# A hybrid attention, DeltaNet and gated-MLP layer on one core: modulation products, load queues and the second norm rearranged

## The chip, the cores and the metric

The kernel runs on one core of one Trainium2 chip. Its time is the device time of one execution in microseconds (us), and the time given for a kernel is the median over several runs. Engines are named as in the profile: PE is TensorE (matmuls, with weight loads as PEld), DVE is VectorE, ACT is ScalarE, POOL is GpSimd, SP is SyncE, which only issues transfers here. SPq and ACTq are the issuing queues of SP and ACT.

## The reference

One layer of a diffusion backbone, on 256 latent tokens x and 256 context tokens ctx of width 2048. A conditioning vector (c for the latents, c_ctx for the context) gives six modulation vectors through one matrix, w_ada (2048 x 12288). What bears on this case:

```python
sh1, sc1, g1, sh2, sc2, g2 = split(silu(c) @ w_ada + b_ada, 6)
csh1, csc1, ...            = split(silu(c_ctx) @ w_ada + b_ada, 6)
lat = modulate(rmsnorm(x, norm_mix), sh1, sc1) @ w_in       # modulate: h * (1 + scale) + shift
con = modulate(rmsnorm(ctx, norm_mix), csh1, csc1) @ w_in
# columns of lat, con feed latent attention (8 heads) and a bidirectional gated DeltaNet (8 heads)
y = (sigmoid(gate_a) * (y_mla @ w_o_mla) + sigmoid(gate_b) * (y_dn @ w_o_dn)) @ w_out
x = x + g1 * y
h = modulate(rmsnorm(x, norm_ffn), sh2, sc2)
gate, val = split(h @ w_ffn_up, 2)                          # hidden width 5504
x = x + g2 * ((silu(conv3(gate)) * val) @ w_ffn_down)
```

Of the modulation, only the first two vectors (shift sh1, scale sc1) are needed for both streams; g1, sh2, sc2 and g2 are needed for the latents alone.

## The kernel before

Activations lie transposed: features on the 128 partitions, tokens along the free axis, so a width of 2048 is 16 tiles (k = 0 to 15) of 128 x 256 per stream. Every large product is done with operands split in two parts of less precision (hi and lo: ACT rounds, DVE subtracts, lines 119 and 120) and three partial products. Weights come from HBM into tiles of tag raw, 128 x 1024 words, of which there are five (NR = 5) for the whole kernel.

**The opening** (lines 313 to 490) computes the first modulated norm H and at the same time the first projection `fp`, seven column groups of w_in (864 columns, `wfirst`), accumulated over k in seven PSUM tiles. It is written out by hand: PE, ACT (`oact`) and DVE (`odve`) keep the order of the program there. SP's loads are issued in the order written, each when its buffer is free.

- `spread` copies silu(c) and silu(c_ctx) to all partitions (`scb`), by 16 matmuls for each stream and copies by DVE (latents) and ACT (context).
- The squares of x and ctx are summed over features on PE (`pss`), gathered (`part`, `msp`), raised to -1/2 on POOL (`rsq`, L171) and spread over partitions by four matmuls (`bc_ps`, then `bc`). Tiles of squares, the output that the DVE reductions throw away (`junk`) and `part` share tag sq, two buffers.
- Shift columns: the 16 feature tiles make 8 pairs. For pair p four raw tiles are loaded (`load_shift`, L333), multiplied on PE with silu(c), silu(c_ctx) as 32 columns (`mod_mm`: 32 matmul instructions, tile `amp`, and an ACT copy `row`), summed into columns by PE and finished with the bias by ACT (`mod_cols`, tile `shs`).
- Scale columns (`aas`): for the pairs in SCP the same way from the `wt` tiles; for the other feature tiles two DVE reductions each (`scale_dot`, one per stream, 128 x 2048) and one ACT instruction (`scale_fin`). `dots` names the tile of the loop behind which each reduction stands. There are three `wt` buffers of 1 MB.
- Tile k of the loop at L461: the product of a pair of columns for two tiles ahead, the rounding of the next weights (`first_hi`), the matmuls of the seven groups (`first_mm`, 42 for each k) with the column sums between them, the reductions, the next tile of H (`h_prep`), then the loads for k + 4. In tile 1 ACT issues a store of the latents' spread vector to HBM (`Sc`, 1 MB).

**The other modulation vectors** (g1, sh2, sc2, g2; `ada_rest`, L258 to 283) are made beside everything that follows: 128 rows of 512 KB (`rawa`, in the five raw tiles), each loaded by SP and reduced by one DVE instruction (L277) against half of the spread vector (`sch`, loaded from `Sc`). The generator is driven by a rate: each step of another stage calls `ada(ns)`, which adds to what is owed, and as long as something is owed the generator goes on by one yield of 1300. At a change of half it yields without work, two times before the load of `sch` and four after it. The rates are ADB (DeltaNet preparation), AD (attention), ADS (scan), WO (per tile of the output projection) and 1000 per tile of the MLP. 32 rows must be done before the output projection's residual (`ada.done` = 1), 96 before the second norm (`while ada.done < 3`, a loop that makes up for what is missing).

**The second norm** (L1360 to 1400): the output projection (`ops`, 16 tiles of 32 matmul pairs) adds up the squares of x1 on DVE (`ssq`, L1373); the sum over partitions, the power and the spread follow as in the opening, all through class `Rms`. `h2_tile` then makes H2 for each k: DVE multiplies by the norm, ACT scales and shifts, ACT rounds, DVE subtracts. The first four tiles of the MLP (`fps`) go through k in quarters, beside h2_tile. From L506 on the order within an engine is set by a planner, apart from a few stretches.

## Time and profile before

| | us |
|---|---|
| median of 3 runs (1857.85 to 1868.06) | 1860.94 |
| the profiled execution, its own time | 1860.39 |
| its span, first to last instruction | 1858.6 |
| PE busy | 1788.5 (96%) |
| DVE busy | 1376.6 (74%) |
| ACT busy | 928.4 (50%) |
| moved by DMA | 419.71 MB, 226 GB/s |

Mean granted clock of PE over the span: 0.990 of full speed. A row of instructions names line, engine, operation, output <- input, count, busy time and mean duration; in a row ordered by time the first number is the start and the second the duration (or the stretch, where instructions are merged), and square brackets give the idle time of the engine before it and what ended it. Lines are those of the kernel; operations that the ordered wrapper issues all carry line 68, so tile names tell them apart. Matmuls are pipelined, so the durations of neighbours overlap.

### The profile page before, as it was taken

The numbers are of one execution on the slowest core, as the hardware profiler recorded it, in microseconds if no ns is written. First come the engines' busy times: TensorE is split into PE (matmuls) and PEld (weight loads), VectorE is DVE, ScalarE is ACT, GpSimd is POOL, SyncE is SP. The second block draws the span as 40 slices with busy tenths as digits, with TensorE's granted clock in tenths as the row PEclk, the third lists the DMA queues.
The fourth block names the chain that finished last, engine by engine and source line by source line (L and its number), as shares of the span: only waits on it lengthen the run. The fifth ranks groups of instructions, "written<-read, shape, count | busy, mean of one in ns | idle before, by whom it ended". The sixth has DMA issues, their size and how long they took to land.

```text
span 1858.6 us, 32954 instructions
## 1 busy us (share of the span) xinstructions
PE 1788.5 (96%) x12386; PEld 1527.4 (82%) x12386; DVE 1376.6 (74%) x2766; ACT 928.4 (50%) x1899; POOL 44.3 (2%) x45
## 2 busy tenths in 40 slices
PE   7899999999999999999999988999999999999999
PEld 4788887888888887778788876888888888888888
DVE  5677889779777876575679888888877788855554
ACT  3335544444666666233346536555555555544443
POOL 0000001000000000000000000000000000000000
PEclk9999999999999999999999998999999999999999
DMA  9992688774677767777757885767766667766663
GB/s 346 342 373 75 178 230 248 202 246 125 207 237 237 224 208 217 260 253 235 244 188 252 293 282 187 251 222 225 224 215 186 211 217 223 263 200 192 196 200 120
DMA packets 195008, 419.71 MB, mean 226 GB/s; under 512 B 61280, under 2 KB 101344, under 8 KB 192416
## 3 DMA queue, kind: packets, MB, share of 16 engines
q1 hardware_dynamic: 167952, 402.39, 67.1%
q10 hardware_dynamic: 26896, 15.21, 2.7%
q8 instruction: 97, 1.59, 0.3%
q14 instruction: 63, 0.52, 0.1%
HBM read 388.57 MB, written 28.84 MB: 225 GB/s over the span
## 4 chain that ended last, share of the span: by engine, by line
PE 54%; DMA 3%; DVE 2%; ACT 1%; issue 1%; POOL 0%; SPq 0%; ACTq 0%; DVEq 0%
PE fps L68 26%; PE dps L68 13%; PE brp L68 5%; PE gtp L68 4%; PE ops L68 3%; DMA rawa<-in_wada 2%; PE op L68 1%; PE kp L68 1%; PE yp L68 1%; DVE wlo L120 1%; DMA raw<-in_wgate 0%; DMA jit<-Vs 0%; DVE rawa L277 0%; DMA yraw<-Ys 0%; DVE S L1284 0%
## 5 line engine op out<-in xcount | busy, mean ns | idle before, releaser
L120 DVE TENSOR_TENSOR wlo<-raw,whi 128x512 fp32r<-128x512 f32 (+1 forms) x940 | 634.0, 686 | 194.5 <-ACT whi L119 185.4
L119 ACT CAST whi<-raw 128x512 fp32r<-128x512 f32 (+1 forms) x940 | 573.9, 619 | 398.4 <-PE dps L68 113.2
L68 PE MATMUL fps<-H,whi 128*128 128x512 f32 x1376 | 481.8, 398 | 5.7 <-DVE H L120 5.7
L68 PE MATMUL fps<-H,wlo 128*128 128x256 f32 x1376 | 374.6, 282 | 0.8 <-DVE wlo L120 0.7
L68 PEld LDWEIGHTS fps<-H,whi 128*128 128x128 f32 x1376 | 253.7, 189 | 62.6 <-issue 5.7
L68 PEld LDWEIGHTS fps<-H,wlo 128*128 128x128 f32 x1376 | 259.2, 188 | 9.4 <-DVE wlo L120 1.9
L68 PE MATMUL gtp<-h,whi 128*128 128x512 f32 x640 | 235.1, 402 | 0.0
L68 PE MATMUL mmp<-h,whi 128*128 128x512 f32 x640 | 228.9, 400 | 0.0
L68 PE MATMUL dps<-GB,whi 128*128 128x512 f32 x560 | 195.9, 391 | 0.0
L277 DVE CUSTOM_DVE_ANT_0 rawa<-rawa,sch 128x1024 f32<-128x1024 f32 x128 | 156.3, 1222 | 49.6 <-DMA rawa<-in_wada 48.6
L68 PE MATMUL gtp<-h,wlo 128*128 128x256 f32 x640 | 175.9, 285 | 1.4 <-DVE wlo L120 1.4
L68 PE MATMUL mmp<-h,wlo 128*128 128x256 f32 x640 | 176.5, 282 | 0.0
L68 PE MATMUL dps<-GB,wlo 128*128 128x256 f32 x560 | 155.3, 282 | 0.0
L68 PEld LDWEIGHTS gtp<-h,whi 128*128 128x128 f32 x640 | 120.7, 189 | 25.5 <-issue 1.2
L68 PEld LDWEIGHTS mmp<-h,whi 128*128 128x128 f32 x640 | 119.1, 188 | 26.2 <-issue 0.4
L68 PEld LDWEIGHTS gtp<-h,wlo 128*128 128x128 f32 x640 | 121.2, 190 | 7.4 <-DVE wlo L120 1.8
L68 PEld LDWEIGHTS dps<-GB,whi 128*128 128x128 f32 x560 | 105.1, 188 | 21.7
L68 PEld LDWEIGHTS mmp<-h,wlo 128*128 128x128 f32 x640 | 120.4, 188 | 2.8 <-issue 0.6
L68 PEld LDWEIGHTS dps<-GB,wlo 128*128 128x128 f32 x560 | 105.9, 189 | 0.6
L68 PE MATMUL fp<-h,gh 128*128 128x256 f32 (+1 forms) x448 | 86.5, 293 | 6.2 <-ACT h L68 5.2
L68 PEld LDWEIGHTS fp<-h,gh 128*128 128x128 f32 (+1 forms) x448 | 70.3, 191 | 12.1 <-ACT h L68 6.4
L496 ACT COPY fx<-fps 128x256 f32<-128x256 f32 x86 | 31.9, 374 | 68.6 <-PE fps L68 68.6
(557 smaller groups left out, 2602.1 us busy)
## 6 DMA issues: line engine op xcount, KB each, us to landing
rawa<-in_wada SPq DMA_DIRECT2D x128, 512.0 KB, 4.6
raw<-in_wgate SPq DMA_DIRECT2D x82, 512.0 KB, 4.3
raw<-in_wval SPq DMA_DIRECT2D x82, 512.0 KB, 4.7
raw<-in_wdown SPq DMA_DIRECT2D x80, 512.0 KB, 4.3
wt<-in_wadas SPq DMA_DIRECT2D x16, 1024.0 KB, 8.0
raw<-in_wadab SPq DMA_DIRECT2D x32, 512.0 KB, 8.1
raw<-in_wgm SPq DMA_DIRECT2D x32, 512.0 KB, 4.8
raw<-in_wgd SPq DMA_DIRECT2D x32, 512.0 KB, 5.2
```

Source lines behind the costliest of these rows:

```text
L68: i = f(*a, **k)
L119: act.copy(hi, raw)
L120: dve.tensor_tensor(out=lo, in0=raw, in1=hi, op=ALU.subtract)
L277: dve.tensor_tensor_reduce(out=w, in0=w, in1=sch, scale=1.0, scalar=0.0, op0=ALU.mult, op1=ALU.add, accum_out=parts[:, h, j : j + 1])
L496: act.copy(out, ps[:M, T:])
```

## The change

In the opening, the order of squares, spreads and reductions is rewritten; a reduction for the second stream writes over its weights instead of a junk tile of tag sq. The product of pair 0 moves ahead of the norm's broadcast. All further products move into the odd tiles of the loop, the scale product at its start and the shift product after the fourth group; four pairs (1, 3, 5, 7) instead of three take the product on PE for the scales, and the host lays out the weights of these pairs accordingly. The shift loads of pairs 1 to 7 are issued by ACT. The store of Sc moves from tile 1 to tile 12, and wt is loaded ahead of the weights of fp in each tile. The second norm sums the last tile's squares on PE instead of on DVE, keeps the scale and the norm in one DVE instruction, and lets ACT write the rounded part at once. The rates ADB, AD and ADS rise, and a change of half takes one and three yields instead of two and four.

```diff
--- before.py
+++ after.py
@@ -29,7 +29,7 @@
 GH = 512
 NR = 5
 NH = 6
-AD = 0.55
+AD = 0.6
 GD0 = 2
 SC = 7500
 ON = 3000
@@ -37,16 +37,16 @@
 CB = 2000
 CC = 7000
 RE = 1.0
-ADS = 0.3
+ADS = 0.4
 OD = 8000
 OC = 4000
 WO = 1500
 IK = 7000
 NW = 3
-SCP = (2, 5, 7)
+SCP = (1, 3, 5, 7)
 R0 = 1.3
 R1 = 1.0
-ADB = 4000
+ADB = 4500
 SCALE = 192.0 ** -0.5
 
 
@@ -265,11 +265,11 @@
             h, j = (n // 16 + c) % 2, n % 16
             if h != half:
 
-                for _ in range(2 if i else 0):
+                for _ in range(1 if i else 0):
                     yield 1300
                 half, sch = h, ad.tile([P, GR], F32, tag="sch", name="sch")
                 sync.dma_start(sch, Sc[h])
-                for _ in range(4):
+                for _ in range(3):
                     yield 1300
             w = ahead
             if i < 127:
@@ -316,21 +316,20 @@
     sel = pa.tile([P, 3], F32, name="sel")
     sync.dma_start(sel, io["sel"])
 
-    def spread():
-        for s in range(2):
-            for q in range(4):
-                bp = psm.tile([P, 4, P], F32, tag="mm", name="scp")
-                for j in range(4):
-                    pe.matmul(bp[:, j], sc[:, 4 * q + j, s : s + 1].broadcast_to([P, P]), ident, start=True, stop=True)
-                (oact.copy if s else odve.tensor_copy)(scb[:, s, q * 512 : q * 512 + 512], bp.rearrange("p a b -> p (a b)"))
+    def spread(s):
+        for q in range(4):
+            bp = psm.tile([P, 4, P], F32, tag="mm", name="scp")
+            for j in range(4):
+                pe.matmul(bp[:, j], sc[:, 4 * q + j, s : s + 1].broadcast_to([P, P]), ident, start=True, stop=True)
+            (oact.copy if s else odve.tensor_copy)(scb[:, s, q * 512 : q * 512 + 512], bp.rearrange("p a b -> p (a b)"))
 
     Sc = dram.tile([2, P, GR], F32, name="Sc")
 
-    def load_shift(p):
+    def load_shift(p, eng):
         raws = []
         for m in range(4):
             raws.append(wr.tile([P, GR], F32, tag="raw", name="raw", bufs=NR))
-            sync.dma_start(raws[m], io["wadab"][p, m])
+            eng.dma_start(raws[m], io["wadab"][p, m])
         return raws
 
     def mod_mm(raws):
@@ -362,9 +361,10 @@
 
     def scale_dot(k, s):
 
+        junk = wts[k]
         if s == 0:
             scm[k] = pa2.tile([P, 2], F32, tag="scm", name="scm")
-        junk = pa2.tile([P, D], mybir.dt.bfloat16, tag="sq", name="junk")
+            junk = pa2.tile([P, D], mybir.dt.bfloat16, tag="sq", name="junk")
         odve.tensor_tensor_reduce(out=junk, in0=wts[k], in1=scb[:, s], scale=1.0, scalar=0.0, op0=ALU.mult, op1=ALU.add, accum_out=scm[k][:, s : s + 1])
 
     def scale_fin(k):
@@ -410,29 +410,46 @@
         ks = slice(4 * q, 4 * q + 4)
         sync.dma_start(xl[:, ks], io["xT"][:, ks])
         sync.dma_start(xc[:, ks], io["ctxT"][:, ks])
-    shift = load_shift(0)
+    shift = load_shift(0, sync)
     grs = {}
     for k in range(3):
         grs[k] = load_first(k)
         if k < 2:
             wts[k + 1] = load_scale(k + 1)
     pe.pinned = True
-    spread()
-    for s in range(2):
-        scale_dot(0, s)
 
     pss = psa.tile([P, 512], F32, tag="aux", name="pss")
-    for k in range(0, KD, 2):
-        sq = pa2.tile([P, 2, 2, T], F32, tag="sq", name="sq")
-        oact.activation(sq[:, :, 0], xl[:, k : k + 2], AF.Square)
-        x2 = xc[:, k : k + 2]
-        if k in (8, 10, 14):
-            odve.tensor_tensor(out=sq[:, :, 1], in0=x2, in1=x2, op=ALU.mult)
+    sqs = {}
+
+    def square(k, s, e):
+        if k not in sqs:
+            sqs[k] = pa2.tile([P, 2, 2, T], F32, tag="sq", name="sq")
+        x = (xl, xc)[s][:, k : k + 2]
+        if e is oact:
+            e.activation(sqs[k][:, :, s], x, AF.Square)
         else:
-            oact.activation(sq[:, :, 1], x2, AF.Square)
+            e.tensor_tensor(out=sqs[k][:, :, s], in0=x, in1=x, op=ALU.mult)
+
+    def square_sum(k):
+        sq = sqs.pop(k)
         for j in range(2):
             g = (k + j) % 4
             pe.matmul(pss[32 * g : 32 * g + 32], ones.broadcast_to([P, 32]), sq[:, j].rearrange("p a b -> p (a b)"), start=k + j < 4, stop=k + j >= KD - 4)
+
+    spread(0)
+    for s in range(2):
+        for k in (0, 2):
+            square(k, s, oact)
+    spread(1)
+    for k in (0, 2):
+        square_sum(k)
+    scale_dot(0, 0)
+    for k in range(4, KD, 2):
+        square(k, 0, oact)
+        square(k, 1, oact if k in (6, 8) else odve)
+        square_sum(k)
+        if k == 4:
+            scale_dot(0, 1)
     part = pa2.tile([P, 512], F32, tag="sq", name="part")
     oact.copy(part, pss)
     msp = psa.tile([P, 4], F32, tag="aux", name="msp")
@@ -442,50 +459,49 @@
     odve.tensor_scalar(out=ms, in0=msp, scalar1=1.0 / D, scalar2=EPS, op0=ALU.mult, op1=ALU.add)
     rsq(pa2, ms, ms, 4)
     scale_fin(0)
+    later = mod_mm(shift)
     bc_ps = psa.tile([P, 512], F32, tag="aux", name="bc_ps")
     for n in range(4):
         pe.matmul(bc_ps[:, n * P : n * P + P], ms[:, n : n + 1].broadcast_to([P, P]), ident, start=True, stop=True)
     bcp = bc_ps.rearrange("p (a b) -> p a b", a=2)
-    later = mod_mm(shift)
     hk = first_hi(0)
     mod_cols(0, False, *later)
     h_prep(0, *hk)
     oact.copy(bc, bcp)
-    shift = load_shift(1)
+    shift = load_shift(1, oact)
     wts[3] = load_scale(3)
     grs[3] = load_first(3)
     first_ps = [(psm if j < 4 else psa).tile([P, 512], F32, tag="mm" if j < 4 else "aux", name="fp") for j in range(2 * N1 + 1)]
 
-    dots = {1: [1, 1], 2: [2, 2], 3: [3, 3], 5: [6, 6], 6: [7], 7: [7, 8], 8: [8, 9], 9: [9], 11: [12, 12], 12: [13], 13: [13]}
+    dots = {1: [1, 1], 3: [4], 4: [4, 5], 5: [5], 6: [8], 7: [8], 8: [9], 9: [9], 10: [12], 11: [12], 12: [13], 13: [13]}
     for k in range(KD):
-        p, later = (k + 2) // 2, None
-        if k > 1 and p < KD // 2:
-            if k % 2 == 0:
-                later = p, False, *mod_mm(shift)
-            elif p in SCP:
-                later = p, True, *mod_mm([wts[2 * p + m // 2][:, m % 2 * GR : m % 2 * GR + GR] for m in range(4)])
+        p = (k + 1) // 2
         nxt = first_hi(k + 1) if k + 1 < KD else None
-        first_mm(k, *hk, 0, 3)
-        if k == 1:
-            later = 1, False, *mod_mm(shift)
-            first_mm(k, *hk, 3, 5)
-        if later:
-            mod_cols(*later)
-        first_mm(k, *hk, 5 if k == 1 else 3, 2 * N1 + 1)
+        if k % 2 and p < KD // 2:
+            if p in SCP:
+                later = mod_mm([wts[2 * p + m // 2][:, m % 2 * GR : m % 2 * GR + GR] for m in range(4)])
+            first_mm(k, *hk, 0, 2)
+            if p in SCP:
+                mod_cols(p, True, *later)
+            first_mm(k, *hk, 2, 4)
+            later = mod_mm(shift)
+            first_mm(k, *hk, 4, 5)
+            mod_cols(p, False, *later)
+            if p + 1 < KD // 2:
+                shift = load_shift(p + 1, oact)
+            first_mm(k, *hk, 5, 2 * N1 + 1)
+        else:
+            first_mm(k, *hk, 0, 2 * N1 + 1)
         for c in dots.get(k + 1, ()):
             scale_dot(c, int(c in scm))
-        if k == 1:
-            shift = load_shift(2)
-        if k > 1 and k % 2 == 0 and k + 4 < KD:
-            shift = load_shift(k // 2 + 2)
         if k + 1 < KD:
             if k + 1 in scm:
                 scale_fin(k + 1)
             h_prep(k + 1, *(hk := nxt))
         if k + 4 < KD:
+            wts[k + 4] = load_scale(k + 4)
             grs[k + 4] = load_first(k + 4)
-            wts[k + 4] = load_scale(k + 4)
-        if k == 1:
+        if k == 12:
             tc.keep_in_program_order(act.dma_start(Sc.rearrange("h p i -> p h i"), scb[:, 0].rearrange("p (h i) -> p h i", h=2)))
     pe.pinned = False
     for s in range(2):
@@ -1369,7 +1385,7 @@
         dve.scalar_tensor_tensor(out=x1[:, f], in0=yx, scalar=adaT[:, f : f + 1], in1=xr[:, f % 2], op0=ALU.mult, op1=ALU.add)
         sq = pd3.tile([P, T], F32, tag="t2", name="x1q")
         act.activation(sq if f else ssq[:, 0], x1[:, f], AF.Square)
-        if f:
+        if 0 < f < KD - 1:
             dve.tensor_tensor(out=ssq[:, 0], in0=ssq[:, 0], in1=sq, op=ALU.add)
         ada(WO)
     dump("x1", x1)
@@ -1377,18 +1393,25 @@
         ada(1)
 
 
-    rms = Rms(pd3, 1, 1)
-    rms.add_sq(ssq)
-    b2 = rms.finish(1.0 / D, None)
+    rms = Rms(pd3, 2, 1)
+    for v in (ssq, sq.unsqueeze(1)):
+        rms.add_sq(v)
+    ms = pd3.tile([P, 2], F32, tag="ms", name="ms", bufs=1)
+    dve.tensor_scalar(out=ms, in0=rms.ss[:, :2], scalar1=1.0 / D, scalar2=EPS, op0=ALU.mult, op1=ALU.add)
+    rsq(pd3, ms, ms, 2)
+    b2 = psa.tile([P, T], F32, tag="aux", name="b2")
+    for n in range(2):
+        pe.matmul(b2[:, n * P : n * P + P], ms[:, n : n + 1].broadcast_to([P, P]), ident, start=True, stop=True)
     a2 = pd.tile([P, KD], F32, name="a2")
     dve.scalar_tensor_tensor(out=a2, in0=adaT[:, 32:48], scalar=1.0, in1=nffn, op0=ALU.add, op1=ALU.mult)
     H2 = hp.tile([P, KD, 2, T], F32R, tag="h", name="H2")
 
     def h2_tile(k):
         h = pd3.tile([P, T], F32, tag="gx", name="h2")
-        dve.tensor_tensor(out=h, in0=b2[:, :T], in1=x1[:, k], op=ALU.mult)
-        act.activation(h, h, AF.Identity, bias=adaT[:, 16 + k : 17 + k], scale=a2[:, k : k + 1])
-        split(h, H2[:, k, 0], H2[:, k, 1])
+        sh = adaT[:, 16 + k : 17 + k]
+        dve.scalar_tensor_tensor(out=h, in0=x1[:, k], scalar=a2[:, k : k + 1], in1=b2, op0=ALU.mult, op1=ALU.mult)
+        act.activation(H2[:, k, 0], h, AF.Identity, bias=sh, scale=1.0)
+        dve.scalar_tensor_tensor(out=H2[:, k, 1], in0=h, scalar=sh, in1=H2[:, k, 0], op0=ALU.add, op1=ALU.subtract)
 
 
     ffn = [(w, f) for f in range(NFF) for w in ("wgate", "wval")]
```

## The prediction

> **What bounds the kernel now.** I read the page first, then a table of stretches, then the waits of TensorE (PE), and last the two stages that the diff touches, in order of time.
>
> ```profile
> span 1858.6 us, 32954 instructions
> PE 1788.5 (96%) x12386; PEld 1527.4 (82%) x12386; DVE 1376.6 (74%) x2766; ACT 928.4 (50%) x1899; POOL 44.3 (2%) x45
> ...
> 1018.00:1101.60 83.60, 83.60 (x479) 73.12 (x478) 67.57 (x126) 44.34 (x88) 0.00 (x0) 1.00 0.82 278
> 1107.30:1124.60 17.30, 1.62 (x20) 1.26 (x21) 15.02 (x34) 6.07 (x13) 0.69 (x1) 0.62 0.84 288
> ```
>
> In a stretch's row stand its length, the busy time of PE, weight loads, VectorE (DVE), ScalarE (ACT) and POOL, the granted clock, the DMA share and GB/s. PE is the bound: 1788.5 of 1858.6 us, and without a gap in the output projection (83.60 of 83.60). So time can come only from PE's 70 us of idleness, from matmuls added or dropped, and from stretches at half clock. Two gaps lie in the diff's reach: the opening, and the 17.3 us around the second norm, where PE works for 1.62.
>
> ```profile
> 25.88 0.58 ACT L68 COPY part<-pss 128x512 f32<-128x512 f32 x1 [1.36 <-PE pss L68]
> 27.27 1.02 POOL L171 TENSOR_TENSOR ms<-ms,half 128x4 f32<-128x4 f32 x1 [25.54 <-DVE ms L68]
> 28.35 1.16 PE L68 MATMUL bc_ps<-ident,ms 128*128 128x128 f32 x8 [1.40 <-POOL ms L171]
> 29.43 3.57 PE L68 MATMUL amp<-raw,csf 128*32 128x256 f32 x32
> 35.03 0.36 PE L68 MATMUL fp<-h,gh 128*96 128x256 f32 x1 [1.22 <-ACT h L68]
> 42.53 0.36 PE L68 MATMUL fp<-h,gh 128*96 128x256 f32 x1
> 79.54 0.36 PE L68 MATMUL fp<-h,gh 128*96 128x256 f32 x1 [3.84 <-ACT h L68]
> 93.97 0.40 PE L68 MATMUL fp<-h,gh 128*96 128x256 f32 x2
> 98.98 1.93 PE L68 MATMUL amp<-raw,csf 128*32 128x256 f32 x32
> 106.42 1.93 PE L68 MATMUL amp<-wt,csf 128*32 128x256 f32 x32
> L68 PE MATMUL fp<-h,gl x224: 277/281/416, 36.0 to 151.5; 128*128 128x256 f32 x96, 128*96 128x256 f32 x16
> 79.50:84.00 4.50, 4.30 (x21) 4.07 (x22) 4.48 (x7) 1.48 (x3) 0.00 (x0) 0.62 0.98 375
> ```
>
> The first projection (fp) runs from 35.0 to about 151.7. A plain tile k takes 5.0 us (93.97 to 98.98), one with a modulation product ahead of it 7.4 (98.98 to 106.42), so a product with its column sums costs 2.45. Sixteen tiles and ten products make 80 + 24.5 = 104.5, so 12.2 us of 116.7 are lost: 2.5 in tile 0 (35.03 to 42.53 for 5.0), 3.84 before 79.54 and about 1.7 after it (4.50 us at a mean clock of 0.62 hold 2.8 us of work), the rest in small pieces.
>
> **The opening, step by step.** (1) *Start of fp.* Squares are shared out anew, the second spread's copies go behind the first squares, and the product of pair 0 moves ahead of the norm's broadcast, so it runs under the 1.02 us of POOL. The squares' sums end at 25.8 now. With one junk tile instead of two competing for the two buffers of tag sq, I put that at 24.0 (bounds 22.5 and 25.8). Then 1.1 for part and column sums as now, the product from 25.1 to 27.0 (1.93 at full clock; 3.57 is what it took here), and 2.0 from its end to fp (33.0 to 35.03 now) plus 0.5, since the broadcast now lies behind it: 29.5, a gain of 5.5. With no gain in the squares and half clock fp starts at 33 (gain 2); at best at 28 (gain 7).
>
> (2) *A fourth scale pair on PE*: +2.45.
>
> ```profile
> L68 DVE CUSTOM_DVE_ANT_0 junk<-wt,scb 128x2048 bf16<-128x2048 f32 x18 | 40.6, 2287 | 8.2 <-DMA wt<-in_wadas 8.2
> ```
>
> With the pairs differently chosen six of the 20 VectorE reductions of 2.3 us go (18 lie in this stretch). But the pair's product stands at the head of tile 1, where PE now waits for VectorE anyway (the 2.5 us of tile 0), so 1.9 of it is covered; without that cover the whole 2.45 counts. Bounds +0.5 and +2.5.
>
> (3) *The Sc store moves from tile 1 to tile 12.*
>
> ```profile
> SPq L333 <- DMA Sc<-scb: 12.0, 1, 12.0
> DVE junk L68 <- DMA wt<-in_wadas: 8.2, 2, 6.5
> ```
>
> SyncE's queue stood 12.0 us behind that store with a shift load at its head; the wt load queued behind came late, VectorE waited 6.5 us for it, and PE the 3.84. Gone with the clock loss: -5.5. At tile 12 every weight of the opening has been asked for, and only the loads of the next stage stand behind it, some 20 us ahead of their use.
>
> (4) *Shift loads issued from ScalarE, four per pair at the odd tile, after the shift columns (tiles 1 to 11).* This is the edit that I fear.
>
> ```profile
> 845.01 0.33 ACTq L864 DMA_DIRECT2D Gs<-zx  x1
> 845.38 3.74 ACT L119 CAST whi<-raw 128x512 fp32r<-128x512 f32 x7 [0.40 <-ACT zx L861]
> ...
> 131.17 0.31 PE L68 MATMUL amp<-sel,row 128*32 128x2 f32 x16
> 131.55 0.41 ACT L68 ACTIVATE shs<-amp,vecs 128x2 f32<-128x2 f32 x2 [1.35 <-PE amp L68]
> 131.85 0.38 ACT L68 ACTIVATE aas<-scm,b,vecs 128x2 f32<-128x2 f32 x1
> 132.79 0.51 ACT L68 ACTIVATE h<-xl,shs 128x256 fp32r<-128x256 f32 x1 [0.55 <-DVE xl L68]
> 41.97 0.51 ACT L68 ACTIVATE h<-xl,shs 128x256 fp32r<-128x256 f32 x1 [0.98 <-DVE xl L68]
> ```
>
> One issue keeps ScalarE idle for 0.40 us though seven casts are ready. Four make 1.6. Behind them on ScalarE stand the scale (aas) and H of the next tile, for which PE waits. From the start of the column sums, T: shs at T+0.38 (131.17, 131.55), issues to about T+2.05, then H, and PE 0.56 after H begins (41.97 to 42.53): T+2.7. Where the scale comes from VectorE's sums (tiles 3, 7, 11), aas and xl stand in between too, 0.94 more (131.85 to 132.79): T+3.6. PE has only groups 5 and 6 left after the sums, 2/7 of 5.0, and runs dry at T+1.7. Three stalls of 1.0 and three of 1.9 make +8.7. Bounds: 0, if the issues pass while ScalarE waits for something else, and 12, if each issue takes half as long again.
>
> [...]
>
> (5) *The rest.* Tile 0 took 7.5 us with two reductions on VectorE, so an even tile with one takes 5.2 against PE's 5.0, six times, half of them under a scale product: +0.5. Writing a reduction over its weights is what L277 does already; I cost it at nothing. Sum of the opening: -5.5 + 0.55 - 5.5 + 8.7 + 0.5 = -1.25. Of the losses in small pieces (some 4 of the 12.2) I let the thinned-out reductions save 1.75, and take -3 (bounds -13 and +3).
>
> **The second norm.**
>
> ```profile
> 1101.29 0.40 PE L68 MATMUL ops<-MB,whi 128*128 128x512 f32 x1
> 1106.90 0.40 PE L68 MATMUL ops<-MB,whi 128*128 128x512 f32 x1
> 1115.93 0.40 PE L68 MATMUL ss<-ones,ssq 128*32 128x1 f32 x16 [8.64 <-DVE ssq L1373]
> 1117.92 1.22 PE L68 MATMUL bc_ps<-ident,ms 128*128 128x128 f32 x4 [1.59 <-POOL ms L171]
> 1124.61 0.76 PE L68 MATMUL fps<-H,whi 128*128 128x512 f32 x1 [5.46 <-DVE H L120]
> ...
> 1105.88 0.42 DVE L497 TENSOR_TENSOR yx<-ops,yx 128x256 f32<-128x256 f32 x1
> 1112.44 0.42 DVE L497 TENSOR_TENSOR yx<-ops,yx 128x256 f32<-128x256 f32 x1
> ...
> 1018.00:1101.60 83.60, 14.69 (x12) 1.00 0.82 278
> 1101.60:1124.60 23.00, 12.20 (x10) 0.71 0.84 282
> ```
>
> The last two rows count the modulation rows (rawa) that VectorE reduces. Ten of them (12.2 us of VectorE, in order) stand around the norm, because the loop up to 96 rows is made up there. I counted the generator's steps with the old and new rates: the owed nanoseconds of each stage by 1300, with the yields at each half. Before, 86 rows are done when the output projection ends (16 at the attention's start, then 35, 22, 13), and ten are missing, which the last row shows. After: 16, 47, 25 and 19, together 107; the ninety-sixth falls in its seventh tile, and no burst is left.
>
> VectorE reached the tile that ended at 1101.7 at 1105.9, 4.2 late; I leave it 4.2 late for the last tile too: yx at 1111.5 instead of 1112.44, then without rows between them x1, the square and the sum at about 1112.9 instead of 1115.93 (-3). ss to the end of the broadcast stays 3.2. Then a tile of H is one VectorE, one ScalarE and one VectorE operation, about 1.7 with hand-overs (0.42 to 0.51 each in the rows above), against 5.5 now behind rows and splits (-3.8): -6.8. Bounds: -10.5 with no lag, -3 with late weights.
>
> **Late rates.** Twelve rows more in attention, three in the scan, six in the output projection, 21 x 1.22 us on VectorE (14.69 for 12); ten leave the burst, the others the MLP.
>
> ```profile
> 500.00:600.00 100.00, 97.41 (x757) 84.78 (x755) 75.96 (x163) 68.18 (x168) 4.59 (x4) 1.00 0.79 249
> DVE rawa L277 <- DMA rawa<-in_wada: 8.0, 7, 2.3
> ```
>
> In attention VectorE is busy for 76%, so the rows find room; each can hold a chain up for 1.2 us where PE's filling tiles (gate projections) don't cover it: +0.5 (0 to 8). The yields at a half's change, four for six, are covered by the same tiles; a late scale row would hold VectorE for the rest of its load.
>
> Sum: -3 - 6.8 + 0.5 = -9.3, from the execution's own 1860.39 us (span 1858.6, 1.8 around it): 1851. The median of the runs, 1860.94, is 0.5 above that execution, so nothing is corrected.
>
> **Rivals.** *The issues cost nothing*: shift columns come early enough, or the four issues overlap; the opening then gives 13 and the time is 1841. For it: no row shows four issues in a line on ScalarE. Against: the 0.40 above. *The opening gives nothing and the norm half*:
>
> ```profile
> 100.00:110.00 10.00, 10.00 (x124) 8.19 (x114) 6.13 (x11) 4.54 (x11) 0.00 (x0) 1.00 0.99 384
> wt<-in_wadas SPq DMA_DIRECT2D x16, 1024.0 KB, 8.0
> raw<-in_wadab SPq DMA_DIRECT2D x32, 512.0 KB, 8.1
> ```
>
> a pair of tiles loads two wt, four raw and two gr of 128 x 864 words, 5.1 MB, and PE asks for that in 13.7 us (10 + 2.45 + half of 2.45), 371 GB/s, where a full stretch moved 384. Shift loads then share with the weights and end late, and 1857 is left. *Slower*: VectorE becomes the bound of the output projection. In its 83.6 us VectorE is busy for 67.6, 14.7 of them on 12 rows; with 18 rows in the same stretch it is 75, and the other 8.7 us cover a DMA wait of 0.48 per row. Seven waits took 8.0 us, 1.1 each. From a mean of 0.48 on, PE runs dry; at 1.1 it loses 18 x 1.1 - 8.7 = 11, 12 over all 16 tiles, and the lag eats the norm's gain: 1860.4 - 3 + 12 + 0.5 = 1870. Against: a late VectorE finds its rows landed, and PE had no gap with 0.8 rows a tile.
>
> **How the numbers follow.** What can be told from no change here is 0.5%, 9.3 us: faster means under 1851.6. The forecast has 0.40 (its own range 1846 to 1857, 0.6 of it under the bound), free issues 0.30, the weak gain 0.20, the slower one 0.10. Faster: 0.24 + 0.29 + 0.02 = 0.55; slower, half of the last and a little, 0.06; the same 0.39. The range of 1839 to 1863 leaves out the far ends of the first and last rival.
>
> **What would show it.** fp starts near 29.5; no wait over 2 us for wt; waits of fp for ACT h at the starts of tiles 2, 4, 6, 8, 10 and 12, 1 and 2 us by turns; fp ends near 149. No row between the last yx and ss; ss about 6 us after the last ops product, fps 4 to 5 after that. PE without a gap from 1010 to the last ops product. Wrong would be: fp's end after 152, or gaps in the output projection.

## The result, and the profile after

The changed kernel takes 1873.2 us (median of 20 runs, 1862.05 to 1882.96), the kernel before 1857.91 (20 runs): ratio 1.0075, 95% interval 1.0058 to 1.0092. It is slower, by 14 us; the forecast was 9 us faster. The profiled execution of the changed kernel, 1862.05 us, is the fastest of its twenty, so its profile shows less than the whole loss; for this reason gains and losses below are taken from ratios over many runs, and profiles only say where.

The page after: the span, and the engines' busy time.

```profile
span 1860.3 us, 33078 instructions
...
PE 1789.5 (96%) x12450; PEld 1531.5 (82%) x12450; DVE 1368.8 (74%) x2758; ACT 922.6 (50%) x1883; POOL 43.1 (2%) x45
```

PE has 64 more matmul instructions and one more busy microsecond. Now the opening: first PE in order of time (start, duration, idle time before it and its releaser), then the products with gl as one group, with shortest, median and longest duration in ns and the first and last start.

```profile
25.57 1.93 PE L68 MATMUL amp<-raw,csf 128*32 128x256 f32 x32
...
29.83 0.36 PE L68 MATMUL fp<-h,gh 128*96 128x256 f32 x1 [1.01 <-ACT h L68]
...
48.48 0.36 PE L68 MATMUL fp<-h,gh 128*96 128x256 f32 x1 [0.91 <-ACT h L68]
...
64.46 0.36 PE L68 MATMUL fp<-h,gh 128*96 128x256 f32 x1 [2.77 <-ACT h L68]
...
81.04 0.36 PE L68 MATMUL fp<-h,gh 128*96 128x256 f32 x1 [1.00 <-ACT h L68]
...
96.06 0.36 PE L68 MATMUL fp<-h,gh 128*96 128x256 f32 x1 [1.80 <-ACT h L68]
...
115.34 0.36 PE L68 MATMUL fp<-h,gh 128*96 128x256 f32 x1 [2.17 <-ACT h L68]
...
130.60 0.36 PE L68 MATMUL fp<-h,gh 128*96 128x256 f32 x1 [2.01 <-ACT h L68]
```

```profile
L68 PE MATMUL fp<-h,gl x224: 277/281/418, 31.2 to 157.3; 128*128 128x256 f32 x96, 128*96 128x256 f32 x16
```

fp starts 5.2 us earlier than before (29.83 against 35.03) and ends 5.8 later (157.3 against 151.5). Six waits for H stand at the starts of tiles 2, 4, 6, 8, 10 and 12, 10.7 us together. ScalarE's side of the second of them:

```profile
60.16 0.33 ACTq L68 DMA_DIRECT2D raw<-in_wadab  x1
...
60.53 2.38 ACTq L68 DMA_DIRECT2D raw<-in_wadab  x3
62.95 0.39 ACT L68 ACTIVATE aas<-scm,b,vecs 128x2 f32<-128x2 f32 x1 [2.39 <-issue]
63.90 0.51 ACT L68 ACTIVATE h<-xl,shs 128x256 fp32r<-128x256 f32 x1 [0.55 <-DVE xl L68]
```

The four issues run from 60.16 to 62.91; the scale (aas) and H stand behind them, and PE starts 0.56 after H. The granted clock after the wait that ended at 96.06 (stretch, its length, PE's busy time, clock, DMA share, GB/s):

```profile
94.00:96.00 2.00, 0.26 (x3) 1.00 0.94 340
96.00:98.00 2.00, 1.77 (x10) 0.82 0.92 348
98.00:100.00 2.00, 2.00 (x11) 0.50 0.76 309
100.00:102.00 2.00, 2.00 (x16) 0.83 0.81 272
```

A wait of 1.80 us is followed by some 3.4 us at half clock (0.18 x 2 + 0.5 x 2 + 0.17 x 2 = 1.7 us of work lost). The same follows the wait before 130.60 (clock 0.65 on average from 132 to 136). The second norm after:

```profile
1124.10 0.31 PE L68 MATMUL ss<-ones,x1q 128*32 128x1 f32 x16 [2.64 <-ACT x1q L1387]
...
1125.46 1.22 PE L68 MATMUL b<-ident,ms 128*128 128x128 f32 x4 [1.06 <-POOL ms L171]
...
1128.41 0.77 PE L68 MATMUL fps<-H,whi 128*128 128x512 f32 x1 [1.73 <-DVE H L1414]
```

From the last ops product (1120.0) to fps are 8.4 us where 17.7 were. So the pause around the norm is some 9 us shorter, but the output projection already ended 13.1 us later than before (1120.0 against 1106.9): 5.8 came out of the opening and 7 between it and the norm. The modulation rows on VectorE, before (first fence) and after (second), in attention's last part and in the scan:

```profile
655.00:720.00 65.00, 8.23 (x7) 1.00 0.61 193
760.00:850.00 90.00, 10.98 (x9) 0.98 0.74 246
```

```profile
655.00:720.00 65.00, 16.87 (x14) 1.00 0.74 241
760.00:850.00 90.00, 17.00 (x14) 0.98 0.78 261
```

### The profile page after: what moved, and what is told of

Its sections match the earlier page's. It is cut to its first block, busy times and chain, and to the rows that moved or that the text cites. A ratio compares the mean times of both kernels' runs of the same rounds, so it can differ in the third digit from the quotient of the medians.

```text
span 1860.3 us, 33078 instructions
## 1 busy us (share of the span) xinstructions
PE 1789.5 (96%) x12450; PEld 1531.5 (82%) x12450; DVE 1368.8 (74%) x2758; ACT 922.6 (50%) x1883; POOL 43.1 (2%) x45
## 4 chain that ended last, share of the span: by engine, by line
PE 48%; issue 9%; DMA 2%; DVE 2%; ACT 1%; POOL 0%; ACTq 0%; POOLq 0%; DVEq 0%; SPq 0%
PE fps L68 26%; PE dps L68 13%; PE gtp L68 4%; PE brp L68 2%; PE op L68 1%; PE yp L68 1%; PE kp L68 1%; DMA rawa<-in_wada 1%; DVE wlo L120 0%; DMA raw<-in_wgd 0%; DMA jit<-Xo 0%; DVE rawa L277 0%; DMA raw<-in_wgate 0%; ACT whi L119 0%; DMA Gs<-zx 0%
## 5 line engine op out<-in xcount | busy, mean ns | idle before, releaser
L68 PE MATMUL fp<-h,gh 128*128 128x256 f32 (+1 forms) x448 | 90.2, 299 | 13.4 <-ACT h L68 11.7
```

The source lines that it names most:

```text
L68: i = f(*a, **k)
```

## The experiments

Theory A: the issues on ScalarE cost the opening its gain. Theory B: the late rates cost the time. Theory C: the shift loads are limited by the DMA engines, whoever issues them. Each run is compared with the kernel before on its own chip. What the runs tell together is this path from one kernel to the other; the us are differences of ratio times 1858, their 95% interval some 5 to 6 us each way (3 for the first).

| step | ratio to before (95%) | step, us | forecast |
|---|---|---|---|
| second norm in fewer steps | 0.9967 (0.9950 to 0.9984) | -6.1 | -6.8 |
| + store of Sc at tile 12 | 0.9931 (0.9907 to 0.9955) | -6.7 | -5.5 |
| + new start | 0.9914 (0.9891 to 0.9937) | -3.2 | -5.5 |
| + new loop of tiles (with the fourth pair and wt loaded first), shift loads by SP | 0.9961 (0.9943 to 0.9979) | +8.7 | -0.7 |
| + late rates | 1.0024 (1.0002 to 1.0047) | +11.7 | +0.5 |
| + shift loads by ACT: the changed kernel | 1.0075 (1.0058 to 1.0092) | +9.5 | +8.7 |

Two of the forecasts split one gain: the 6.8 for the norm hold 3.0 for modulation rows that leave its pause, and these go only with the late rates. Like for like the forecasts are -3.8 for the norm and -2.5 for the late rates.

Two runs outside this path agree with it: the opening alone has 1.0044 (1 plus the path's four steps there: 1.0045), the rates alone 1.0063 (1 plus the path's step: 1.0063).

### Who issues the shift loads

```diff
-    shift = load_shift(1, oact)   ...   if p + 1 < KD // 2: shift = load_shift(p + 1, oact)
+    shift = load_shift(1, sync)   ...   if p + 1 < KD // 2: shift = load_shift(p + 1, sync)
```

> The changed kernel with one thing undone: the 28 shift loads of pairs 1 to 7 are issued by SyncE again, in the same place of the program. Theory A (the four issues in a row on ScalarE hold up the scale and H behind them; PE runs dry six times, 10.7 us in the changed kernel's profile, and two of the stalls are followed by stretches at half clock, some 4 us): the waits of fp for ACT h shrink under 3 us in all, the first projection ends near 144 instead of 157, and the time falls by 10 to 14 us, to 1859 to 1863 against 1873. Theory C (the shift loads share the DMA engines with the weights, whoever issues them): PE waits as long, now for raw or wt, fp ends at 155 or later, time within 3 us of 1873. Theory B (the late rates cost the time): the opening may gain, but the median stays over 1868.

Measured: 1864.5 us, ratio 1.0024 (1.0002 to 1.0047), 9.5 us under the changed kernel. PE's waits in the opening:

```profile
PE amp L68 <- DMA wt<-in_wadas: 2.8, 1, 2.8
PE fp L68 <- ACT h L68: 2.0, 5, 1.0
```

Waits for H fall from 11.7 (seven) to 2.0, fp ends at 146.4. A holds for the waits, and its time is missed by 1.5 us; C falls, in the changed kernel's loop. But 4.5 us of loss remain.

The same issues, one place further on, still on ScalarE:

```diff
-            if p + 1 < KD // 2: shift = load_shift(p + 1, oact)    # ahead of aas, H
+            if k % 2 and (k + 3) // 2 < KD // 2: shift = load_shift((k + 3) // 2, oact)    # behind h_prep(k + 1)
```

> The changed kernel with the four issues moved on ScalarE's own queue to behind the scale and H of the next tile (pairs 2 to 7; rates and norm stay changed). Theory A (it is the place of the issues ahead of H that stalls PE): PE's waits of fp for ACT h fall from 11.7 to under 4 us, fp ends at 146 to 149, time as with SyncE's loads, 9 us under the changed kernel, ratio to before 1.001 to 1.004. Rival (ScalarE is late because of the issues wherever they stand, now with the cast of the next weights and the copy of the sums behind them): waits of 8 us or more, fp ends after 153, ratio over 1.005.

Measured: 1863.6, ratio 1.0029 (1.0011 to 1.0048); fp ends at 149.4.

```profile
PE amp L68 <- DMA raw<-in_wadab: 4.9, 5, 2.0
PE fp L68 <- ACT h L68: 1.8, 4, 1.0
```

The waits for H go as with SP's loads: what cost was the place of the issues ahead of H. Issued later, some loads land late (4.9).

Then the issues on ScalarE in the old loop, with the store moved and the new norm (0.9931 without them):

```diff
-    def load_shift(p):          ...  sync.dma_start(raws[m], ...)
+    def load_shift(p, eng=oact):  ...  eng.dma_start(raws[m], ...)      # pair 0 stays with sync
```

> The old opening with the store of Sc at tile 12 and the new norm (ratio 0.9931, fp ends at 143.4), with one thing changed: the 28 shift loads of pairs 1 to 7 are issued by ScalarE, at the old places in the loop (after the reductions of an even tile, ahead of H). Theory I (four issues hold ScalarE for 1.3 to 2.8 us wherever H stands behind them, and PE has no more than 1.7 us left): waits of fp for ACT h of 1 us and more in six tiles, fp ends 5 to 10 us later, ratio 0.996 to 0.999. Rival J (in the old loop the columns are made a tile ahead, so that ScalarE issues while PE has most of a tile's groups left): waits under 4 us in all, ratio 0.992 to 0.995.

Measured: 1865.0, ratio 1.0025 (1.0009 to 1.0042), 17.5 us over the same kernel with SP's loads; fp ends at 161.6 instead of 143.4. Neither theory: H waits little, as J says, and the time is lost all the same.

```profile
PE amp L68 <- DMA raw<-in_wadab: 12.7, 8, 4.5
PE fp L68 <- ACT h L68: 3.5, 3, 1.6
```

The loads come late. First the rows of this kernel (ACT's queue, then PE), then SP's queue in the kernel that leaves the loads to SP:

```profile
47.06 0.26 ACT L68 ACTIVATE shs<-amp,vecs 128x2 f32<-128x2 f32 x1 [1.48 <-PE amp L68]
47.07 0.33 ACTq L68 DMA_DIRECT2D raw<-in_wadab  x1
...
47.50 1.52 ACTq L68 DMA_DIRECT2D raw<-in_wadab  x3
```

```profile
53.08 0.81 PE L68 MATMUL amp<-raw,csf 128*32 128x256 f32 x8 [4.47 <-DMA raw<-in_wadab]
```

```profile
41.10 4.61 SPq L333 DMA_DIRECT2D raw<-in_wadab  x4
```

SP asks for pair 2 from 41.1 on and has asked for all of it by 45.7, ACT begins at 47.07: on ScalarE the issue stands in line behind shs, which itself waits for PE. So an issue on ScalarE costs twice here: its own time ahead of what follows (60.16 to 62.91 for four in the changed kernel), and the lateness of what precedes (47.07 instead of 41.10). In the new loop the first decides, in the old one the second.

### The opening's other parts

The new opening whole, with old rates and old norm:

```diff
-AD = 0.6, ADS = 0.4, ADB = 4500, yields 1 and 3, second norm as changed
+AD = 0.55, ADS = 0.3, ADB = 4000, yields 2 and 4, second norm as before
```

> The changed kernel with old rates and old second norm: the opening alone. Theory A: it costs the 5.8 us by which fp ends later (157.3 against 151.5) and what the half-clock stretches add, time 1863 to 1868 against 1858. Rival (the opening's loss is made up later, since the loads of the next stage come earlier relative to PE): the gate products end within 2 us of those of before, time 1856 to 1860. If the opening costs 10 or more, the half-clock stretches of most executions are longer than in the profiled one, which was the fastest of its twenty.

Measured: 1868.5, ratio 1.0044 (1.0030 to 1.0058): +8.2 us. The top of A's range; the gate products end 5.2 us late (968.2 against 963.0), nothing is made up.

New opening with SP's loads, new norm, old rates:

```diff
-changed kernel
+the same with load_shift(p + 1, sync) and the old rates and yields
```

> The changed kernel with old rates and with the shift loads issued by SyncE: second norm in fewer steps plus the opening without its issues on ScalarE. If the parts add: the norm alone measured 0.9967 of the time before (-6.1 us), and the opening with SyncE's loads ended fp at 146.4 against 151.5 (-5.1): 1849 against 1860, ratio 0.994 (0.992 to 0.996). Rival (a gain of the opening is lost again in attention and scan, where other steps then meet other loads): time as with the norm alone, 0.9965 or more.

Measured: 1850.1, ratio 0.9961 (0.9943 to 0.9979). It beats both kernels, yet it is only 1 us better than the norm alone (give or take 5), just outside both ranges and nearer to the rival's: the opening gives about nothing, though fp starts at 29.6 and no issue stands on ScalarE. So each part of the opening by itself. First the store, with the old opening and the new norm:

```diff
-        if k == 1:
+        if k == 12:
             tc.keep_in_program_order(act.dma_start(Sc..., scb...))
```

> The kernel before with the new second norm and one line more: the store of Sc after tile 12 instead of tile 1; the opening is else the old one. My forecast gave the store's move -5.5 us (3.84 of PE's wait, 1.7 of half clock). If right: ratio 0.9967 with the norm alone goes to 0.9935 to 0.9945, time 1847, and fp ends 5 us earlier, at 146. Rival (the weights come late anyway, since the loads of the opening already take most of what the DMA engines move, and the wait shows up in another tile): fp ends within 2 us of 150.6, ratio 0.996 to 0.9975.

Measured: 1848.4, ratio 0.9931 (0.9907 to 0.9955); fp from 33.5 to 143.4. The step of my sum holds: -6.7 us for one line (give or take 5.5), and the loads don't give the wait back.

Then the new start ahead of the old loop:

```diff
-new loop (products in odd tiles, four pairs on PE), load_shift(..., oact), late rates
+old loop (products two tiles ahead, three pairs), load_shift(..., sync), store at tile 12, old rates
```

> The new start (squares shared out anew, second spread behind the first squares, product of pair 0 ahead of the broadcast, one junk tile) before the old loop of tiles (products for pair p two tiles ahead in even tiles, three scale pairs, shift loads from SyncE), the store of Sc at tile 12, new norm, old rates. Theory L (the new loop's order loses, the start's gain is real): fp from 29.6 to 140, time 4 to 5 us under the same without the new start (ratio 0.9931), 0.990 to 0.992. Rival W (the loads set the pace: they move 410 GB/s up to the first tiles, so an earlier start only waits earlier, for wt or raw): fp ends at 143 or later, ratio 0.9925 to 0.995.

Measured: 1842.1, ratio 0.9914 (0.9891 to 0.9937); fp from 29.9 to 141.6. It is the fastest of all, 16 us under the kernel before and 30 under the changed one by the ratios. Against the same kernel without the new start that is -3.2, with an interval of about 6 either way, and fp ends 1.8 earlier; by the middle values L's ratio holds and both of W's marks fail, but the interval covers L and W. The run does say what the new loop costs: 8.7 us. Is it the fourth pair?

```diff
-SCP = (1, 3, 5, 7);  dots = {1: [1, 1], 3: [4], 4: [4, 5], ...}
+SCP = (2, 5, 7);     dots = {1: [1, 1], 2: [2, 2], 3: [3, 3], 5: [6, 6], ...}    # new loop, SP's loads, old rates, new norm
```

> The new norm and the new opening with SyncE's loads and old rates (ratio 0.9961), but with three scale pairs on TensorE as before (2, 5 and 7, and their old order of VectorE's reductions) in place of four. Theory P (the fourth pair's product costs PE 2.45 us and a wait for its two weights at tile 1, 4.7 us in that kernel's profile): fp ends 3 to 7 us earlier than 148.1, ratio 0.993 to 0.9945. Rival (VectorE's two reductions in each of tiles 1 to 3 then hold up H, as in the kernel before): waits of fp for ACT or DVE h grow by as much, ratio 0.9955 or more.

Measured: 1854.6, ratio 0.9969 (0.9951 to 0.9987), 1.5 us over four pairs, within the interval; fp ends at 151.0 in this profile. The rival's numbers hold. PE's waits in the opening, four pairs in the new loop, three pairs in the new loop, three pairs in the old loop:

```profile
PE amp L68 <- DMA wt<-in_wadas: 4.7, 1, 4.7
PE fp L68 <- ACT h L68: 1.8, 4, 1.0
```

```profile
PE fp L68 <- ACT h L68: 7.4, 9, 1.8
PE fp L68 <- DVE h L68: 2.1, 9, 0.8
```

```profile
PE amp L68 <- DMA raw<-in_wadab: 1.8, 3, 0.6
PE fp L68 <- ACT h L68: 1.5, 3, 1.0
```

The last two have the same start, the same pairs, the same order of reductions and SP's loads; they differ in the loop's order alone, in products and loads, and by 10 us (0.9969 against 0.9914). So the reductions, which the rival blamed, are not enough. In the new loop a pair's shift columns are made in the tile just ahead of their first use, in the old one a tile earlier, and PE's waits for H are 7.4 against 1.5. VectorE's waits point the same way: for the scale (aas), which ScalarE makes behind the shift columns, 15.8 us against 4.7, and for ScalarE's H 15.0 against 2.8. With four pairs the early product waits instead for its weights, which stand on SP's queue behind shift loads that wait for their buffers (the load goes out at 29.1 us; at 23.4 in the changed kernel, where ACT issues the shift loads). Which of products and loads weighs more was not tried.

### The second norm

```diff
-    rms = Rms(pd3, 1, 1); rms.add_sq(ssq); b2 = rms.finish(1.0 / D, None); h2_tile: multiply, scale and shift, round, subtract
+    the second norm of the changed kernel, nothing else
```

> The kernel before with the second norm in fewer steps and nothing else (old opening, old rates). The ten late modulation rows still stand ahead of the norm, so only the steps behind them are shortened. Theory N (each step removed is removed from the path): PE's pause around the norm falls from 17.3 us to 10 to 13, time 1851 to 1854 against 1858. Rival (the rows set the end of the sum, and H's split was hidden behind the weights of the MLP): pause over 15, time 1856 or more.

Measured: 1853.1, ratio 0.9967 (0.9950 to 0.9984): -6.1 us, with the rows still ahead of it (8.6 us of VectorE in the pause). The pause goes from 17.7 to 13.7 (1103.4 to 1117.1), a little above N's range; the other 2 us of the gain lie within the interval:

```profile
1110.31 0.39 PE L68 MATMUL ss<-ones,x1q 128*32 128x1 f32 x16 [4.57 <-ACT x1q L1371]
...
1112.93 1.22 PE L68 MATMUL b<-ident,ms 128*128 128x128 f32 x4 [2.23 <-POOL ms L171]
...
1117.08 0.77 PE L68 MATMUL fps<-H,whi 128*128 128x512 f32 x1 [2.93 <-DVE H L1398]
```

### The late rates

```diff
-AD = 0.55; ADS = 0.3; ADB = 4000; yields 2 and 4
+AD = 0.6;  ADS = 0.4; ADB = 4500; yields 1 and 3
```

> The kernel before with the late rates alone (AD .6, ADS .4, ADB 4500, three and one yields at each half). Theory B (more rows on VectorE and in the DMA queue in attention, scan and output projection cost PE time there, and the burst they save before the norm is worth less): last product of the output projection 7 to 10 us later than the 1107 of before, the norm's pause shorter by some 5, time 1860 to 1864 against 1858. Rival (as in my prediction, the rows fit into VectorE's idle time): the output projection ends within 2 us of 1107, and the time falls by about 4, to 1854.

Measured: 1872.0, ratio 1.0063 (1.0040 to 1.0085): +11.7 us, the largest loss of the path, above even B's range. The pause falls by 8.5 (1122.4 to 1131.6), so by these numbers some 20 us are lost elsewhere. In the two profiles attention (first gate product to first kp) takes 320.5 us instead of 311.1, and the scan (first kp to last gate product) 216.0 instead of 206.6. The scan shows one way (VectorE, PE, in order of time, in this kernel):

```profile
782.38 0.66 PE L68 MATMUL kp<-S,jit 128*64 128x128 f32 x8
...
783.84 1.22 DVE L277 CUSTOM_DVE_ANT_0 rawa<-rawa,sch 128x1024 f32<-128x1024 f32 x1
...
784.98 0.60 DVE L1248 SCALAR_TENSOR_TENSOR r<-kp,negc,jit 128x128 f32<-128x128 f32 x2
...
785.38 0.44 PE L68 MATMUL kp<-S,jit 128*64 128x128 f32 x4 [2.34 <-DVE r L1248]
```

kp is ready at 783.0; a row takes VectorE from 783.84 until 785; r comes after it, and PE waits 2.34 us. Nothing waits for the row, but r stands behind it. Those waits between 760 and 965 us (total, how often, the longest) and the stretch of the scan's first half (busy times of PE, PEld, DVE, ACT and POOL, then clock, DMA share and GB/s), first in this kernel, then in the one before:

```profile
PE kp L68 <- DVE r L1248: 6.0, 6, 2.3
```

```profile
760.00:850.00 90.00, 83.29 (x508) 64.75 (x507) 58.68 (x146) 24.50 (x50) 0.00 (x0) 0.89 0.70 234
```

```profile
PE kp L68 <- DVE r L1248: 1.2, 2, 0.9
```

```profile
760.00:850.00 90.00, 83.79 (x561) 66.01 (x559) 59.91 (x149) 30.14 (x60) 0.00 (x0) 0.98 0.74 246
```

PE is busy for as long in both, but at a clock of 0.89 instead of 0.98: 8 us of work lost in 90. How much of that is the rates, one profile of each can't say: with old rates, new norm and moved store this stretch has 0.94, in the changed kernel's profile 0.98.

Attention shows another way, and it is not VectorE. ScalarE makes ksq, for which PE waits, and zx, for which it doesn't; first in this kernel, then in the one before:

```profile
476.11 0.51 ACT L885 ACTIVATE zx<-zx,onh 128x256 f32<-128x256 f32 x1 [0.49 <-DVE zx L884]
...
477.02 0.60 ACT L978 ACTIVATE ksq<-kps 128x512 f32<-128x512 f32 x1 [0.40 <-ACT zx L885]
```

```profile
478.96 0.58 ACT L978 ACTIVATE ksq<-kps 128x512 f32<-128x512 f32 x1
...
479.91 0.52 ACT L885 ACTIVATE zx<-zx,onh 128x256 f32<-128x256 f32 x1
```

With late rates the planner has put zx ahead of ksq, and PE's wait is 3.4 us instead of 1.9. It is 1.9 in all eleven profiles with attention's old rates (AD, ADB and the yields) and 3.4 in all seven with the late ones. So a rate doesn't only add rows, it also moves other work.

The rates apart: first the scan's alone, then all the others.

```diff
-ADS = 0.3
+ADS = 0.4
```

> The kernel before with one number changed: ADS .4 for .3, more modulation rows in the scan. Theory S (rows between the scan's steps hold up r on VectorE, for which kp and yp wait in a chain, and each gap can trip the half clock): from the first kp to the gate products' end +4 to +9 us, nothing before the scan, norm's pause shorter by some 3, time +3 to +6, ratio 1.002 to 1.003. Rival T (the loss of the rates lies in attention, and the scan's is only rows shifted by it): within 2 us of before.

Measured: 1867.8, ratio 1.0051 (1.0030 to 1.0071). From the first kp to the last gate product 212.1 us instead of 206.6, as S says; but the time is above its range, and attention is 5 us longer too, a stretch that this rate doesn't touch (clock 0.96 from 560 to 655). Nor do the 212.1 show the rate by themselves: a kernel with old rates that comes below (rows loaded two ahead) has 212.2.

```diff
-AD = 0.55; ADB = 4000; yields 2 and 4
+AD = 0.6;  ADB = 4500; yields 1 and 3
```

> The kernel before with the other rates: AD .6, ADB 4500 and three and one yields, ADS as before. Theory T (attention is where they cost): first kp later by 5 to 9 us against before, scan unchanged, norm's pause shorter by some 5, ratio 1.002 to 1.005. Theory S (the scan is what costs): first kp within 3 us, ratio 0.997 to 1.000. Should the scan be longer here too, with its own rate unchanged, then it is which rows stand between its steps and not how many that decides.

Measured: 1864.6, ratio 1.0051 (1.0032 to 1.0070). The first kp is at 764.1 instead of 756.4, the scan's kp take 168.0 instead of 169.1: T, and nothing in the scan. That attention pays shows in every profile: between the first gate product and the first kp PE is idle for 8.1 to 13.4 us in the eleven with attention's old rates and for 15.5 to 19.3 in the seven with the late ones. What the scan's rate costs in the scan is less sure, as said.

Each of the two runs costs 9.5 us net, both rates together 11.7 and not 19 (each give or take some 4). They shorten one pause (17.7 to 12.1, 10.4, and 9.2 with both), and that would make the two together dearer than their sum, not cheaper; why they are cheaper stays open.

Is it VectorE's time, or the rows' loads? Rows shortened, with old and with late rates:

```diff
-tensor_tensor_reduce(out=w, in0=w, in1=sch, ...)
+tensor_tensor_reduce(out=w[:, :64], in0=w[:, :64], in1=sch[:, :64], ...)
```

> The kernel before, with each late modulation row reduced over its first 64 columns only: the other 960 are left out of the sums, so that a row still loads 512 KB and keeps its waits, but costs VectorE about 0.15 us in place of 1.22. It is the base for the next run. 128 rows x 1.07 us leave VectorE, most of them off the path; the ten rows ahead of the second norm (12.2 us) go from PE's pause. Expected 1846 to 1853 against 1858.

> The same shortened rows (960 of 1024 columns left out of the sums) with the late rates of the change. With whole rows the late rates cost 11.7 us beside the old ones. Theory V (VectorE's 1.22 us a row between the steps of attention and scan is what costs): with short rows late and old rates agree within 3 us. Theory D (the rows' loads cost: 512 KB each in front of the loads that attention and scan wait for, on the same queue): the late rates cost 8 us or more with short rows too, and, since no burst of VectorE is left to be saved, perhaps more than 11.7.

Measured: 0.9926 (0.9901 to 0.9952) and 0.9955 (0.9931 to 0.9979). The late rates cost 5.4 us here, give or take 6.6, against 11.7 with whole rows, give or take 4.2; neither V's bound nor D's is met, and the two costs are not told apart. A row takes 0.22 us here. kp waits for r as long as with old rates (from 445 to 1010 us 2.7 there, and with late rates):

```profile
PE kp L68 <- DVE r L1248: 2.8, 9, 0.7
```

But in attention PE's idle time grows from 8.1 to 15.7 us, no less than with whole rows, and the wait for ksq is 3.4 us here too. So what PE's idle time there gains does not come from VectorE's 1.22 us a row. That leaves the moved work and the rows' loads: VectorE's waits for rawa from 445 to 1125 us grow from 34.2 to 59.1 us. Next I tried that wait, during which a row holds VectorE too:

```diff
-half, ahead = None, load(0)                ...  ahead = load(i + 1)
+half, ahead = None, [load(0), load(1)]     ...  ahead.append(load(i + 2))
```

> The kernel before with its late modulation rows loaded two ahead in place of one, from the same five buffers. Theory W (VectorE standing in line for a row's load is part of what a row costs): the 33 us of waits for rawa between 445 and 1125 fall under 10 us, time 0 to 4 us under 1858. Rival B (a second buffer held by rows is missing for the weights, whose casts then start later): time the same or up to 6 us more, ratio 1.000 to 1.003.

> The same with the late rates. With one row ahead the late rates cost 11.7 us. Theory W: with two ahead they cost 5 to 8 us, what the 1.22 us of the rows alone make. Theory V alone (only the reduction counts): 10 to 13 us as before. Rival B (the weights are short of a buffer, more so with more rows): 13 us or more.

Measured: 1.0005 (0.9985 to 1.0025) and 1.0042 (1.0027 to 1.0057). The late rates cost 6.9 us, give or take 4.6, in W's range but not to be told from 11.7; and W's ground is not there: VectorE stands in line for rawa as long as ever. Its waits from 445 to 1125 us with late rates are 33.7 us in all (28, the longest 3.4) one row ahead and 30.5 (28, the longest 3.3) two ahead.

So the edit didn't do what it was made for, and how the rates' cost divides into loads, moved work and clock stays open.

## Why the prediction was wrong, point by point

The sum was -9.3, measured is +14. Two terms make 21 of the 23 us between them.

*Start of fp, -5.5.* The step is right (29.83 against 29.5 forecast), its worth is unclear: -3.2, not to be told from zero or from -5.5.

*A fourth pair, +0.55, even tiles, +0.5, and small losses, -1.75: the term that failed in the opening.* I costed the new loop as -0.7 and it costs +8.7, with SP's loads. I asked what each product costs on PE, and took the cover from the old profile ("PE now waits for VectorE anyway"). That was a misreading: of the 2.5 us of tile 0 some 1.7 are a lower clock (0.61, 0.50, 0.50 and 0.69 in the four us from 36 on), and at the head of tile 1 PE waits 0.16 us, since H comes just then. With SP's loads the fourth pair's product even waits, 4.7 us for its weights. I did not ask when a product's inputs land and when its columns are used. The old loop made columns a tile ahead of H; the new one has no such slack, and it asks for the weights of pair 1 at tile 1. That the number of pairs is not the cause the run with three pairs shows; that the loop's order is, its comparison with the old loop.

*The store moved, -5.5.* Right: -6.7. My sign for it, no wait over 2 us for wt, was not met in the changed kernel: one of VectorE's two waits for wt is 3.9 us, 5.8 together.

*Shift loads from ScalarE, +8.7.* Right in mechanism, place and size: six stalls, 0.91, 2.77, 1.00, 1.80, 2.17 and 2.01 for 1.0 and 1.9 by turns (the 2.17 stands where 1.0 was due); 9.5 us. The forecast left out the half clock that follows two of them (1.7 us each). The first rival, free issues, falls. A single issue takes 0.33 to 0.44 us in the changed kernel's profile, beside 6.7 from issue to landing; what decided was four of them beside the 1.7 us of slack that I had estimated for PE: the last three took 1.35 to 2.55 us.

*The second norm, -6.8.* Right. The shorter steps alone take 4.0 us from the pause, where 3.8 were forecast for them, and 6.1 by the ratio (give or take 3). With the rows gone as well the pause is 9.3 us shorter, where 6.8 were forecast.

*Late rates, +0.5 (0 to 8): the term that failed most.* +11.7, outside my bounds, although the shorter pause is already in it. The rows were counted right: 49 instead of 37 in attention, 23 instead of 20 in the scan. I argued from a share: VectorE is busy for 76% in attention, so the rows find room. They find room, but in the scan a row that stands between kp and r holds PE up by as much as 2.3 us (6.0 us in all instead of 1.2), though VectorE is busy for only 58.7 of 90 us there. I wrote that "each can hold a chain up for 1.2 us", and then took the value at the bottom of the range. In attention I took the order of all other work as given; it changes with the rates, PE's idle time there grows with short rows too, and ksq is 1.5 us of it. And I did not price a lower clock (0.89 instead of 0.98 from 760 to 850 us, in one profile of each). The burst of ten rows that the rates save cost 8.5 us in one place; spread out, the rows and what came with them cost some 20. That the forecast took room on VectorE for room in the plan is shown; how the 20 us divide is open.

*The slower rival*, VectorE as the bound of the output projection, has its sign right and its place wrong. PE loses 2.4 us there in two gaps, not 12:

```profile
PE ops L68 <- DVE wlo L120: 2.4, 2, 1.6
```

*The weak gain* put the loss on shared DMA engines. With the store moved alone, 110 us suffice for fp (33.5 to 143.4) with the same bytes, so in the old loop they don't set the pace.

## What to carry to other kernels

A side job's instruction is priced by what stands behind it in the queue, not by its engine's idle share: PE waited 2.34 us where one row of 1.22 us stood ahead of r, with VectorE busy for 58.7 of 90. Here one pause in which the main engine stands anyway was a better place for ten such instructions (8.5 us) than between the steps of other stages (some 20 us, with what came with the rows). Where a planner sets the order, compare the order of the other engines too: changing a rate moved work that has nothing to do with the rows. The same holds for a transfer's issue: on ScalarE four of them delayed H (11.7 us of PE's waits in the changed kernel, 2.0 with SP's loads), and in the old loop they were themselves delayed by shs (47.07 instead of 41.10). Before products are moved, ask for each when its inputs land and how many tiles ahead of its use it is made: the slack does not show as a cost until it is gone.

## What the runs showed of the hardware

In the changed kernel's opening PE has six waits for H of 0.91 to 2.77 us. Those of 1.80 and 2.01 were followed by some 3.4 us at half clock (0.82, 0.50 and 0.83 in the rows from 96 to 102; 0.85 from 130 to 132 and 0.65 from 132 to 136). The other four, those of 2.77 and 2.17 among them, were not (1.00 from 48 to 54, 64 to 70, 81 to 87 and 115 to 121). So the length of the wait alone doesn't decide it; what does, these profiles don't show.

The spread of the changed kernel's runs goes mostly with this clock. Mean granted clock and time go together over its 20 runs (correlation -0.86): 1862.05 us at 0.990, 1882.96 at 0.980, 20.9 us for 0.010, where 0.010 of the time is 18.7. With the mean clock c, I estimate what it costs as time x (1 - c) at most: 24.5 us on average before (29 runs), 28.6 in the changed kernel, 30.3 with the late rates alone, 22.3 with the new norm, 20.3 in the fastest kernel. By these numbers some 6 of the 12 us of the late rates may come as lower clock; without the scan's rate it is 2 of 9.5 (24.6 against 22.5 before on that chip), so the share is not settled. And one profile, which may meet few slow stretches, can hide most of a loss: that of the changed kernel shows 1.7 of the 14 us (1862.05 against 1860.39).
